# Last projection of a decoder layer: sixteen of twenty-two feature blocks by seven products of quarters, placed between the tiles of the projection before it

## The chip, the core and the metric

The kernel is one launch on one core of a Trainium2 chip. The core has a tensor engine (PE) for matmuls, with its weight loads (PEld) shown apart, a vector engine (DVE), a scalar or activation engine (ACT), a general engine (POOL) and a queue (SP) that issues the transfers between the chip's main memory and on-chip memory. Each engine works through its own list of instructions in the order in which they were issued; semaphores tie the lists together. The metric is device time in microseconds (us); lower is better.

## What is computed

One decoder layer on 512 tokens of width 1024, in float32: a gated mixer of three branches, and then a channel mixer (`conv_ffn`) whose two projections make up the last third of the kernel. The change concerns the second of these, `@ w_down`.

```python
def conv_ffn(u, w_up, conv_w, conv_b, w_down):
    h = causal_dwconv(u @ w_up, conv_w, conv_b)
    a, v = h[..., :D_FF], h[..., D_FF:]           # D_FF = 2816 = 22 blocks of 128
    return (jax.nn.silu(a) * v) @ w_down          # [512, 2816] @ [2816, 1024]

x = x + merged @ w_o[i]                           # the residual
x = x + conv_ffn(rmsnorm(x, ln2_g[i]), ...)
return rmsnorm(x, final_g)
```

## The kernel before

**Products in three parts.** Every float32 matrix is split into a high part (a cast by ACT, `fp32r`) and a low part (the rest, a subtraction by DVE). `mm3` (L230) then makes high x high, high x low, and low x high, in this order, over all the blocks of the contraction: 3 matmuls for each block. For a projection the tokens' block of 128 is loaded as weights and 512 columns stream past it.

**Jobs.** All work is cut into jobs, one tile of a weight matrix each. The program is written out by a generator; its order is the order on every engine. Before job n is issued, `prepare` (L1588) issues the low part of the weights of job n+1 (`lows`, L211, on DVE, then the job's `then`, if it has one), the cast of those of job n+2 (`cast`, L191, on ACT, in two halves, each at one of the job's steps), and the transfer of those of job n+3 (`fetch`, L179, on SP). There are 2 buffers for raw weights, 3 for high parts, 2 for low parts. A job calls `step()` at fixed places, usually twice; each step advances every generator in the list `running` by one stage. That is how work that belongs to an earlier tile gets laid between later ones.

**First projection of the channel mixer** (`up_jobs`, 22 jobs, numbered 0 to 21; even ones for a, odd ones for v, two blocks each, two products of 24 matmuls). `up_evac` takes each block out: ACT scales it (L1162), DVE adds the two taps of the convolution (L1165), ACT applies the silu to a (L1167), and POOL multiplies a and v (L1170). `later` then splits the result into its two parts, over the following steps. For the blocks below KS it makes more: each pair of blocks (2p, 2p+1) of tokens in two halves is a 2 x 2 matrix of quarters, and `sums_of` (L318 to L328) makes the four sums of quarters that seven products need, in three stages: four adds on DVE, two casts on ACT, two subtractions on DVE (`sl` or `sal`, then `sbl`). The sums are kept in `FS`, the plain parts in `ACTS`.

**Second projection** (`down`). For blocks 0 to 7 (KS = 8), seven products of quarters stand for eight, as in Strassen's method in Winograd's form. Four quarters of weights are read; differences of them (`diff`, L333) form the other three. The products, 24 matmuls each, are mixed with the plain jobs for blocks 8 to 21 (`blocks_of`). The products' results are added to one another and to the residual tiles `X1` (L1229, L1250, L1264, L1269, L1270). All of this runs after the last up job. `put_x1` writes the residual to main memory after up job 3, and `get_x1` reads it back before `down`.

**Memory.** `big` holds 54 tiles of 128 x 512 for everything in passing, PSUM has 4 banks under the name `mm` and 4 under `sm`.

Of the kernel before, what the change touches and what calls it, by code (L numbers as in the profile page):

```python
# [10 lines left out]
F32 = mybir.dt.float32  # L11
F32R = mybir.dt.float32r
# [4 lines left out]
P = 128  # L17
S = 512
# [10 lines left out]
SH = 16  # L29
DFF = 2816  # L30
KF = DFF // P
KS = 8
C_Q, C_K, C_V = 0, AW, 2 * AW
C_POOL = 3 * AW
C_Z = C_POOL + D
# [48 lines left out]
def trunk(ctx: ExitStack, tc, out, x, rel_bias, ln1_g, w_in, b_gate, w_a, pool_w, pool_scale, w_b,  # L84
# [26 lines left out]
    def MM(name):  # L111
        return psum.tile([P, S], F32, name=name, tag="mm")
# [970 lines left out]
                t = X1[tb, h] = T("x1")  # L1083
                sp.dma_start(t, x[tb * P:(tb + 1) * P, h * S:(h + 1) * S])

    def put_x1():
        nxt["x1"] = dram.tile([4, 2, P, S], F32, name="x1d")
        for tb, h in X1:
            sp.dma_start(nxt["x1"][tb, h], X1[tb, h])

    def get_x1():
        back = upool.tile([P, KD, S], F32, name="x1b", tag="ul")
        for h in range(2):
            for tb in range(4):
                X1[tb, h] = back[:, 2 * tb + h, :]
                sp.dma_start(X1[tb, h], nxt["x1"][tb, h])

    def wo_jobs(pair, h):
        def evac(tb, ps):
            t = X1[tb, h]  # L1100
# [33 lines left out]


    ACTS = {}
    wide = []
    ff = {}

    def ff_cols():  # L1140
# [19 lines left out]
    def up_evac(m, ps):  # L1160
        t = HC[m] = T("hc")
        act.activation(t, ps, AF.Identity, bias=ff["c1"][:, ff["b"] + m:ff["b"] + m + 1], scale=fw(2, m))  # L1162
        for k in range(2):
            sh = 2 - k
            dve.scalar_tensor_tensor(t[:, sh:], ps[:, :S - sh], fw(k, m), t[:, sh:], OP.mult, OP.add)  # L1165
        if m < KF:
            act.activation(t, t, AF.Silu)  # L1167
            return
        a = HC[m - KF]
        pool.tensor_tensor(a, a, t, OP.mult)  # L1170

        def later():
            yield
            k = m - KF
            if k >= KS or k % 2:
                h, l = T("fh", F32R), T("fl", F32R)
                act.copy(h, a)
                dve.tensor_sub(l, a, h.bitcast(F32))
                ACTS[k] = (h, l)
                if k < KS:  # L1180
                    yield
                    for _ in sums_of(HC[k - 1], a, *(t[:, k // 2, :] for t in wide),
                                     lambda j, h, l: FS.__setitem__((j, k // 2), (h, l))):
                        yield
                return
            if k == 0:
                wide.extend(ypool.tile([P, 4, S], F32R, name=n, tag="xs") for n in ("sh", "sl"))
            t = T("f0", F32R)
            act.copy(t[:, :256], a[:, :256])
            dve.tensor_sub(t[:, 256:], a[:, :256], t[:, :256].bitcast(F32))  # L1190
            FS[0, k // 2] = (t[:, :256], t[:, 256:])

        running.append(later())

    FS = {}

    def down():

        n2 = KS // 2
        quarter = lambda two, h: w_down[:KS * P, h * S:(h + 1) * S].rearrange(
            "(k two p) c -> two p k c", two=2, p=P)[two]
        W, acc, rs, r3 = {}, {0: {}, 1: {}}, {}, {}

        def load_w():
            both = upool.tile([P, KD, S], F32, name="w3", tag="uh")
            for at in range(2):
                W[at] = both[:, 4 * at:4 * at + 4, :]
                sp.dma_start(W[at], quarter(at, 1))  # L1210
            get_x1()

        def product(ps, ws, parts, first, last):

            wh, wl = ws
            mm3(ps, lambda k: wh[:, k, :], lambda k: wl[:, k, :], lambda k: parts[k][0],
                lambda k: parts[k][1], range(n2), first, last, flip=True)

        def first_half(i):
            return [[t[:, i * P:(i + 1) * P] for t in FS[0, p]] for p in range(n2)]  # L1220

        def second_half(tb):
            return [[t[:, tb * P:(tb + 1) * P] for t in ACTS[2 * p + 1]] for p in range(n2)]

        def sums(j, i):
            return [[t[:, i * P:(i + 1) * P] for t in FS[j, p]] for p in range(n2)]

        def add(tb, h, what):
            dve.tensor_tensor(X1[tb, h], X1[tb, h], what, OP.add)  # L1229

        def job(parts, use, form=None, ld=None):
            def body(ws):
                for i in range(2):
                    use(i, ws)
                    step()
            j = Job(parts, n2, S, body)
            j.form, j.load = form, ld
            return j


        def p2(i, ws):
            acc[0][i] = MM("pb")
            product(acc[0][i], ws, second_half(i), True, False)

        def p1(i, ws):
            ps = SM("p1")
            product(ps, ws, first_half(i), True, True)
            add(i, 0, ps)
            rs[i] = T("r1")
            act.copy(rs[i], ps)  # L1250
            if i:
                diff(W[0], W[1], W[0])

        def p5(i, ws):
            ps = SM("p5")
            product(ps, ws, sums(1, i), True, True)
            add(i, 1, ps)
            add(2 + i, 1, ps)

        def p7(i, ws):  # L1260
            ps = SM("p7")
            product(ps, ws, sums(3, i), True, True)
            r3[i] = T("r3")
            act.copy(r3[i], ps)  # L1264

        def p6(i, ws):
            ps = SM("p6")
            product(ps, ws, sums(2, i), True, True)
            dve.tensor_tensor(rs[i], rs[i], ps, OP.add)  # L1269
            dve.tensor_tensor(r3[i], r3[i], rs[i], OP.add)  # L1270

            def rest():
                yield
                add(2 + i, 0, r3[i])
                yield
                add(i, 1, rs[i])
                yield
                add(2 + i, 1, r3[i])
            running.append(rest())

        def p4(i, ws):
            product(acc[0][2 + i], ws, second_half(2 + i), False, True)
            add(2 + i, 0, acc[0][2 + i])
            running.append(early(2 + i))

        def p3(i, ws):
            acc[1][i] = SM("pb")
            product(acc[1][i], ws, sums(4, i), True, False)

        one = job([quarter(0, 0)], p1)  # L1290
        five = job([], p5, lambda: diff(one.raw, W[0], one.raw), lambda: None)
        def formed():
            diff(W[1], W[1], one.raw)
            return W[0]

        seven = job([], p7, formed, lambda: None)
        six = job([], p6, lambda: W[1], lambda: None)
        four = job([quarter(1, 0)], p4, lambda: diff(four.raw, four.raw, W[1]))
        plain = blocks_of(0, acc[0], (0, 1), (2, 3))

        yield Call(load_w)
        yield job([quarter(1, 0)], p2)
        yield next(plain)
        yield one
        yield five
        yield next(plain)
        yield seven
        yield next(plain)
        yield six
        yield from plain  # L1310
        yield four
        yield job([quarter(1, 1)], p3)
        yield from blocks_of(1, acc[1], (0, 1), ())

    def up_jobs():
        held = []
# [52 lines left out]
        yield  # L1369
        fin[tb] = norm_early(X1[tb, 0], fin["g"])  # L1370

    def blocks_of(h, acc, opened, keep):
        def evac(tb, ps):
            t = X1[tb, h]
            dve.tensor_tensor(t, t, ps, OP.add)
            if h == 0:
                running.append(early(tb))
                return
            v0, xg0 = fin[tb]
            for _ in norm_late(t, fin["g"], v0, lambda xg1: ((xg1, xg1), (xg0, xg0))):  # L1380
                xg1 = _
            for i, o in ((1, xg1), (0, xg0)):
                sp.dma_start(out[tb * P:(tb + 1) * P, i * S:(i + 1) * S], o)

        return jobs_b(lambda k0, k1: [wsrc(w_down, KS + k0, KS + k1, h * S, h * S + S)], S,
                      lambda k, tb: ACTS[KS + k][0][:, tb * P:(tb + 1) * P],
                      lambda k, tb: ACTS[KS + k][1][:, tb * P:(tb + 1) * P], KF - KS, evac,
                      mk=(MM, SM)[h], tail=2 if h else 0, acc=acc, opened=opened, keep=keep)


    class Call:
# [3 lines left out]
    def program():  # L1395
# [34 lines left out]
        for pair in range(2):  # L1430
            for h in range(2):
                yield from wo_jobs(pair, h)
            if pair == 0:
                yield Call(ff_cols)
        for i, job in enumerate(up_jobs()):
            yield job
            if i == 3:
                yield Call(put_x1)
        yield Call(lambda: fin.setdefault("g", grow(final_g)))
        yield Call(finish)  # L1440
        yield from down()

    jobs = list(program())
    weights = [j for j in jobs if isinstance(j, Job)]
# [166 lines left out]
ORDERED = {EngineType.PE, EngineType.Activation, EngineType.DVE, EngineType.Pool}  # L1611
NBIG = 54
MORE = 2
SPLIT = 4
MIX = "ZZ0zz1ggggaa"
SSD_ORDER = ((0, 0, 1), (1, 0, 1), (0, 1, 1), (2, 0, 1), (1, 1, 1), (3, 0, 1), (2, 1, 1), (3, 1, 1))
# [30 lines left out]
```

## Time and profile before

| | us |
|---|---|
| median of 3 runs | 1051.29 (1051.25 to 1051.93) |
| the profiled execution, as timed | 1052.9 |
| its span in the profile | 1050.8 |
| PE busy | 1037.0 (99%), 5220 matmuls |
| DVE busy | 642.9 (61%) |
| ACT busy | 467.4 (44%) |
| POOL busy | 137.7 (13%) |
| up jobs on the chain, from 699.47 | 229.42 |
| weights' low parts on DVE, L211 | 218.6 (95 instructions) |
| weights' high parts on ACT, L191 | 189.6 (188 instructions) |

Times in a row of the profile are microseconds from the start of the span, unless a row says ns. A row in order of time gives start, length, engine, line, operation, what is written and from what, and how many instructions are merged; in brackets how long the engine stood idle before it and on whom it waited. Where rows of one engine follow closely, they overlap a little in their ends: the distance from start to start is what an instruction costs in a dense row. A row by stages gives the stage, its length, the busy time of PE, PEld, DVE, ACT and POOL with counts, the clock granted to PE (1.00 is full), the share of the transfer engines and GB/s.

### The profile page before, as it was taken

What the parts mean: (1) busy time and instruction counts of PE and PEld (TensorE: products, weight loads), DVE (VectorE), ACT (ScalarE), POOL (GpSimd) and SP (SyncE); (2) the same over time, 40 slices, a digit from 0 to 9 for tenths busy, and PEclk for the clock granted to TensorE, in tenths of its full rate; (3) what the DMA queues carried; (4) which work ended last, traced back from release to release, by engine and by line L of the source; (5) the groups of instructions that cost most, each with busy time, mean ns of one, the idle gap of its engine ahead of it and who ended that gap; (6) DMA issues with size and microseconds to landing.
All of it is one profiled execution on the core that took longest, in us unless ns stands there. A gap on an engine that the chain in (4) does not pass through costs nothing.

```text
span 1050.8 us, 13095 instructions
## 1 busy us (share of the span) xinstructions
PE 1037.0 (99%) x5220; PEld 864.9 (82%) x5220; DVE 642.9 (61%) x867; ACT 467.4 (44%) x753; POOL 137.7 (13%) x118
## 2 busy tenths in 40 slices
PE   8999999999999999999999999999999999999997
PEld 8888877898888887787887888898888888878885
DVE  5563565675356657576658856766766556556545
ACT  5432544343474363566554324545444443433331
POOL 1670000000000001100143500001111111110110
PEclk9999999999999999999999999999999999999999
DMA  7544312026322354641252426653232322362322
GB/s 241 156 125 136 113 49 74 31 56 182 104 80 81 80 149 112 151 121 52 79 147 85 150 91 220 205 161 119 81 119 82 107 94 82 119 240 67 114 100 80
DMA packets 119787, 121.80 MB, mean 116 GB/s; under 512 B 5523, under 2 KB 101590, under 8 KB 119727
## 3 DMA queue, kind: packets, MB, share of 16 engines
q1 hardware_dynamic: 119727, 120.98, 37.4%
q8 instruction: 41, 0.67, 0.3%
q14 instruction: 19, 0.16, 0.0%
HBM read 115.07 MB, written 4.32 MB: 114 GB/s over the span
## 4 chain that ended last, share of the span: by engine, by line
PE 94%; DVE 3%; DMA 1%; ACT 1%; issue 1%; POOL 0%; SPq 0%; DVEq 0%; ACTq 0%; POOLq 0%
PE pa L230 32%; PE pu L230 22%; PE pb L230 17%; PE pqk L230 9%; PE pa L1507 2%; PE p L230 2%; PE ps L656 1%; PE pu L1329 1%; PE po L695 1%; PE pt L683 1%; PE ppw L230 1%; DVE wl L211 1%; PE py L955 1%; DMA raw<-in_w_in_dram 1%; PE pyo L961 1%
## 5 line engine op out<-in xcount | busy, mean ns | idle before, releaser
L211 DVE TENSOR_TENSOR wl<-raw,wh 128x2048 fp32r<-128x2048 f32 (+3 forms) x95 | 218.6, 2302 | 80.3 <-ACT wh L191 42.3
L191 ACT CAST wh<-raw 128x1024 fp32r<-128x1024 f32 (+3 forms) x188 | 189.6, 1026 | 68.5 <-DVE raw L333 21.1
L230 PE MATMUL pa<-uh,wh 128*128 128x512 f32 x384 | 98.8, 399 | 0.0
L1165 DVE SCALAR_TENSOR_TENSOR hc<-pu,fcol,hc 128x510 f32<-128x510 f32 x88 | 65.9, 748 | 50.8 <-ACT hc L1162 49.2
L230 PE MATMUL pa<-uh,wl 128*128 128x512 f32 x384 | 95.0, 390 | 0.3 <-DVE wl L211 0.3
L230 PE MATMUL pa<-ul,wh 128*128 128x512 f32 x384 | 95.0, 390 | 0.0
L230 PEld LDWEIGHTS pa<-uh,wl 128*128 128x128 f32 x384 | 72.0, 188 | 15.6 <-DVE wl L211 0.7
L230 PEld LDWEIGHTS pa<-ul,wh 128*128 128x128 f32 x384 | 72.1, 188 | 15.2
L230 PE MATMUL pu<-uh,wh 128*128 128x512 f32 (+1 forms) x352 | 83.7, 380 | 0.0
L230 PE MATMUL pu<-uh,wl 128*128 128x512 f32 (+1 forms) x352 | 83.5, 380 | 0.0
L230 PE MATMUL pu<-ul,wh 128*128 128x512 f32 (+1 forms) x352 | 83.5, 380 | 0.0
L230 PEld LDWEIGHTS pa<-uh,wh 128*128 128x128 f32 x384 | 70.2, 188 | 15.2 <-issue 1.0
L230 PEld LDWEIGHTS pu<-uh,wh 128*128 128x128 f32 x352 | 64.1, 188 | 12.7 <-ACT uh L448 0.2
L230 PEld LDWEIGHTS pu<-ul,wh 128*128 128x128 f32 x352 | 64.2, 188 | 12.5
L230 PEld LDWEIGHTS pu<-uh,wl 128*128 128x128 f32 x352 | 64.2, 188 | 12.5
L1162 ACT ACTIVATE hc<-pu,fcol,fcol 128x512 f32<-128x512 f32 x40 | 31.2, 779 | 75.4 <-PE pu L230 75.2
L1170 POOL TENSOR_TENSOR hc<-hc 128x512 f32<-128x512 f32 x22 | 31.5, 1430 | 223.5 <-DVE hc L1165 169.3
L934 POOL TENSOR_TENSOR xd<-xc,dec 128x512 f32<-128x512 f32 x6 | 6.4, 1063 | 364.0 <-DVE xc L925 345.4
L677 ACT ACTIVATE sb<-sb,nm 128x128 f32<-128x128 f32 (+1 forms) x72 | 30.1, 419 | 22.9 <-DVE nm L674 17.2
L1050 ACT ACTIVATE sg<-pa,col 128x512 f32<-128x512 f32 x24 | 16.5, 687 | 51.8 <-PE pa L230 51.7
L230 PE MATMUL pqk<-uh,wh 128*128 128x512 f32 x144 | 36.9, 394 | 0.0
L230 PE MATMUL pqk<-ul,wh 128*128 128x512 f32 x144 | 36.3, 390 | 0.0
(343 smaller groups left out, 1752.4 us busy)
## 6 DMA issues: line engine op xcount, KB each, us to landing
raw<-in_w_in_dram SPq DMA_DIRECT2D x25, 1024.0 KB
raw<-in_ffn_w_up_dram SPq DMA_DIRECT2D x22, 1024.0 KB
raw<-in_w_in_dram SPq DMA_DIRECT2D x20, 512.0 KB
raw<-in_ffn_w_down_dram SPq DMA_DIRECT2D x10, 1024.0 KB
raw<-in_w_o_dram SPq DMA_DIRECT2D x8, 1024.0 KB
raw<-in_w_b_dram SPq DMA_DIRECT2D x4, 1024.0 KB
al<-ad SPq DMA_DIRECT2D x16, 256.0 KB
raw<-in_w_c_dram SPq DMA_DIRECT2D x4, 1024.0 KB
```

Source lines behind the costliest of these rows:

```text
L191: act.copy(job.high[:, :, o], job.raw[:, :, o])
L211: (eng or dve).tensor_tensor(l[:, :, o], job.raw[:, :, o], h[:, :, o].bitcast(F32), OP.subtract)
L230: pe.matmul(ps, l, r, start=first and n == 0, stop=last and n == total - 1)
L656: pe.matmul(pss[i][:, o:o + w * P], q[r, n * P:(n + 1) * P], k[r, kb * P:(kb + w) * P], start=True, stop=True)
L677: act.activation(sb[:, off:off + w * P], sb[:, off:off + w * P], AF.Exp, bias=nm[:, n, h:h + 1], accum_out=ls[:, n, h:h + 1])
L683: pe.transpose(pt[:, o:o + P], sb[:, o:o + P], eye)
L695: pe.matmul(po[DH * hh:DH * hh + DH, n * P:(n + 1) * P], V[g, kb + i][:, (2 * c + hh) * DH:(2 * c + hh + 1) * DH], probs[2 * c + hh, nb][: ...
L1050: act.activation(s, ps, AF.Sigmoid, bias=col[:, o:o + 1])
L1162: act.activation(t, ps, AF.Identity, bias=ff["c1"][:, ff["b"] + m:ff["b"] + m + 1], scale=fw(2, m))
L1165: dve.scalar_tensor_tensor(t[:, sh:], ps[:, :S - sh], fw(k, m), t[:, sh:], OP.mult, OP.add)
L1170: pool.tensor_tensor(a, a, t, OP.mult)
L1507: pe.matmul(first[2 * n + j][:, lo:hi], a[:, k, j * P:(j + 1) * P], b[:, k, lo:hi], start=a is wh and b is uh and k == 0, stop=a is wl and ...
```

## The change

KS becomes 16: blocks 0 to 15 go by seven products, in two groups of eight blocks, and six blocks (16 to 21) stay plain. `down` is replaced by `down_group`, which makes one group's jobs. They are no longer put behind the up jobs: the list `AT` says after which up job each of them runs. Group 0 (blocks 0 to 7): product three after up job 9, seven after 10, one after 11, five after 12, six after 13, two and A22 after 14. Group 1 (blocks 8 to 15): after 17, 18, 19, 20, 21, and the last two after the first plain job. Each product's result is added in full to the residual tiles, from its own banks; `rest` spreads twelve of these adds over the steps behind six. The weights W are read three up jobs ahead of three into two buffers of `ypool`. The sums' parts get tiles of `big` instead of the two wide ones. `put_x1` and `get_x1` are gone: the residual stays in its eight tiles. The plain jobs are those for six blocks: for each half one job of four blocks and one of two.

```diff
-KS = 8
+KS = 16
...
-    def put_x1():
...
-    def get_x1():
...
                 if k < KS:
                     yield
-                    for _ in sums_of(HC[k - 1], a, *(t[:, k // 2, :] for t in wide),
+                    for _ in sums_of(HC[k - 1], a, T("sah", F32R), T("sal", F32R),
                                      lambda j, h, l: FS.__setitem__((j, k // 2), (h, l))):
                         yield
...
-    def down():
+    def down_group(base):
+        quarter = lambda two, h: w_down[base * P:(base + 8) * P, h * S:(h + 1) * S].rearrange(
             "(k two p) c -> two p k c", two=2, p=P)[two]
+        W, r1, r2, r5, r7 = [], {}, {}, {}, {}
+        def side(j):
+            ks = range(base, base + 8, 2)
+            if j == "A11":
+                return [FS[0, k // 2] for k in ks]
+            if j == "A12":
+                return [[t[:, LO] for t in ACTS[k + 1]] for k in ks]
+            if j == "A22":
+                return [[t[:, HI] for t in ACTS[k + 1]] for k in ks]
+            return [FS[j, k // 2] for k in ks]
+        def load():
+            for two in range(2):
+                W.append(ypool.tile([P, 4, S], F32, name="w3", tag="xs"))
+                sp.dma_start(W[two], quarter(two, 1))
...
+        def job(j, raw, form, use):
             def body(ws):
+                wh, wl = ws
+                parts = side(j)
                 for i in range(2):
+                    ps = SM("pd")
+                    o = slice(i * P, (i + 1) * P)
+                    mm3(ps, lambda k: wh[:, k, :], lambda k: wl[:, k, :],
+                        lambda k: parts[k][0][:, o], lambda k: parts[k][1][:, o], range(4), flip=True)
+                    use(i, ps)
                     step()
...
+        def keep(r, name):
+            def use(i, ps):
+                r[i] = T(name)
+                act.copy(r[i], ps)
+            return use
+        def p1(i, ps):
+            keep(r1, "r1")(i, ps)
             add(i, 0, ps)
+        def p5(i, ps):
+            keep(r5, "r5")(i, ps)
+            dve.tensor_tensor(r2[i], r2[i], ps, OP.add)
+        def p6(i, ps):
+            dve.tensor_tensor(r1[i], r1[i], ps, OP.add)
             def rest():
                 yield
+                dve.tensor_tensor(r7[i], r7[i], r1[i], OP.add)
+                add(i, 1, r1[i])
                 yield
+                add(i, 1, r2[i])
+                add(2 + i, 0, r7[i])
                 yield
+                add(2 + i, 1, r7[i])
+                add(2 + i, 1, r5[i])
             running.append(rest())
+        def then1():
+            diff(W[0], W[0], one.raw)
+            dve.tensor_tensor(W[1], W[1], one.raw, OP.add)
+        one = job("A11", quarter(0, 0), None, p1)
+        two = job("A12", quarter(1, 0), None, lambda i, ps: add(i, 0, ps))
+        three = job(4, None, lambda: W[1], keep(r2, "r2"))
+        three.then = lambda: diff(W[1], W[1], W[0])
+        one.then = then1
+        two.then = lambda: diff(two.raw, two.raw, W[1])
+        return load, [[three], [job(3, None, lambda: W[1], keep(r7, "r7"))], [one],
+                      [job(1, None, lambda: W[0], p5)], [job(2, None, lambda: W[1], p6)],
+                      [two, job("A22", None, lambda: two.raw, lambda i, ps: add(2 + i, 0, ps))]]
...
+        loads, groups = zip(*(down_group(base) for base in range(0, KS, 8)))
+        between = {at: group.pop(0) for group, ats in zip(groups, AT) for at in ats}
         for i, job in enumerate(up_jobs()):
             yield job
-            if i == 3:
-                yield Call(put_x1)
+            for load, ats in zip(loads, AT):
+                if i == ats[0] - 3:
+                    yield Call(load)
+            yield from between.get(i, ())
         yield Call(lambda: fin.setdefault("g", grow(final_g)))
         yield Call(finish)
-        yield from down()
+        plain = down_jobs(0)
+        yield next(plain)
+        yield from between.get(2 * (KF // 2), ())
+        yield from plain
+        yield from down_jobs(1)
...
+AT = ((9, 10, 11, 12, 13, 14), (17, 18, 19, 20, 21, 22))
```

More of the change, by code (lines that the diff above doesn't have):

```diff
@@ L1084, in load_x1 @@
                 sp.dma_start(t, x[tb * P:(tb + 1) * P, h * S:(h + 1) * S])
-    def put_x1():
-        nxt["x1"] = dram.tile([4, 2, P, S], F32, name="x1d")
-        for tb, h in X1:
-            sp.dma_start(nxt["x1"][tb, h], X1[tb, h])
-    def get_x1():
[L1092 to L1096, printed above, removed]
     def wo_jobs(pair, h):
@@ L1136, in trunk @@
     ACTS = {}
-    wide = []
     ff = {}
@@ L1185, in later @@
                 return
-            if k == 0:
-                wide.extend(ypool.tile([P, 4, S], F32R, name=n, tag="xs") for n in ("sh", "sl"))
             t = T("f0", F32R)
@@ L1195, in trunk @@
     FS = {}
-    def down():
-        n2 = KS // 2
-        quarter = lambda two, h: w_down[:KS * P, h * S:(h + 1) * S].rearrange(
+    def down_group(base):
+        quarter = lambda two, h: w_down[base * P:(base + 8) * P, h * S:(h + 1) * S].rearrange(
             "(k two p) c -> two p k c", two=2, p=P)[two]
[L1204 to L1226, printed above, removed]
@@ L1228, in add @@
         def add(tb, h, what):
             dve.tensor_tensor(X1[tb, h], X1[tb, h], what, OP.add)
-        def job(parts, use, form=None, ld=None):
+        def job(j, raw, form, use):
             def body(ws):
+                wh, wl = ws
+                parts = side(j)
                 for i in range(2):
-                    use(i, ws)
-                    step()
[L1236 to L1243, printed above, removed]
@@ L1245, in p1 @@
-        def p1(i, ws):
-            ps = SM("p1")
-            product(ps, ws, first_half(i), True, True)
-            add(i, 0, ps)
[L1249 to L1270, printed above, removed]
+                    ps = SM("pd")
[3 more added lines that the diff above has]
+                    use(i, ps)
@@ new lines, in body @@
+                    step()
+            new = Job([raw] if raw is not None else [], 4, S, body)
+            new.form = form
+            if raw is None:
+                new.load = lambda: None
+            return new
+        def keep(r, name):
[5 more added lines that the diff above has]
+            keep(r1, "r1")(i, ps)
+            add(i, 0, ps)
+        def p5(i, ps):
+            keep(r5, "r5")(i, ps)
+            dve.tensor_tensor(r2[i], r2[i], ps, OP.add)
@@ L1272, in rest @@
+        def p6(i, ps):
+            dve.tensor_tensor(r1[i], r1[i], ps, OP.add)
             def rest():
                 yield
-                add(2 + i, 0, r3[i])
+                dve.tensor_tensor(r7[i], r7[i], r1[i], OP.add)
+                add(i, 1, r1[i])
                 yield
-                add(i, 1, rs[i])
+                add(i, 1, r2[i])
+                add(2 + i, 0, r7[i])
                 yield
-                add(2 + i, 1, r3[i])
+                add(2 + i, 1, r7[i])
+                add(2 + i, 1, r5[i])
@@ L1279, in p6 @@
             running.append(rest())
[L1281 to L1311, printed above, removed]
@@ L1312, in down @@
-        yield job([quarter(1, 1)], p3)
-        yield from blocks_of(1, acc[1], (0, 1), ())
+        def then1():
[7 more added lines that the diff above has]
+        two.then = lambda: diff(two.raw, two.raw, W[1])
@@ L1370, in early, with down_jobs @@
         fin[tb] = norm_early(X1[tb, 0], fin["g"])
-    def blocks_of(h, acc, opened, keep):
+    def down_jobs(h):
         def evac(tb, ps):
@@ L1387, in blocks_of @@
                       lambda k, tb: ACTS[KS + k][1][:, tb * P:(tb + 1) * P], KF - KS, evac,
-                      mk=(MM, SM)[h], tail=2 if h else 0, acc=acc, opened=opened, keep=keep)
+                      mk=(MM, SM)[h], tail=2 if h else 0)
     class Call:
@@ L1434, in program @@
                 yield Call(ff_cols)
+        loads, groups = zip(*(down_group(base) for base in range(0, KS, 8)))
+        between = {at: group.pop(0) for group, ats in zip(groups, AT) for at in ats}
         for i, job in enumerate(up_jobs()):
             yield job
-            if i == 3:
-                yield Call(put_x1)
+            for load, ats in zip(loads, AT):
+                if i == ats[0] - 3:
+                    yield Call(load)
+            yield from between.get(i, ())
         yield Call(lambda: fin.setdefault("g", grow(final_g)))
-        yield Call(finish)
-        yield from down()
+        plain = down_jobs(0)
[3 more added lines that the diff above has]
+        yield from down_jobs(1)
     jobs = list(program())
```

## The prediction

> **What bounds the kernel now.** I read the page's first two parts, then the chain that ended last, then the vector engine's queue in order of time through one pair of up jobs, and last the places where the tensor engine stands still.
>
> ```profile
> span 1050.8 us, 13095 instructions
> ...
> PE 1037.0 (99%) x5220; PEld 864.9 (82%) x5220; DVE 642.9 (61%) x867; ACT 467.4 (44%) x753; POOL 137.7 (13%) x118
> ...
> PE 94%; DVE 3%; DMA 1%; ACT 1%; issue 1%; POOL 0%; SPq 0%; DVEq 0%; ACTq 0%; POOLq 0%
> ```
>
> The tensor engine (PE) bounds everything: it is idle for only 14 us. A matmul fewer is worth its full pitch, and every wait that reaches PE costs its full length. From the chain:
>
> ```profile
> 699.47 229.42 PE pu L230 x1056
> 928.89 5.46 PE pb L230 x24
> 934.38 2.25 DVE wl L211
> 936.67 9.36 PE pb L230 x40
> ...
> 967.79 5.44 PE p L230 x24
> ```
>
> The up jobs run without a gap; one product of quarters (24 matmuls) takes 5.44 us, so a matmul's pitch is 0.227 and an up job of 48 takes 10.88. The question is whether the vector engine (DVE), in strict order, can feed products put between up jobs. Its load in two pairs of up jobs, one with sums of quarters and one without (columns: PE, weight loads, DVE, ACT, POOL busy, clock, DMA):
>
> ```profile
> 743.00:765.00 22.00, 22.00 (x99) 18.22 (x98) 15.06 (x18) 10.42 (x15) 2.89 (x2) 1.00 0.31 98
> ...
> 831.00:853.00 22.00, 22.00 (x98) 18.21 (x97) 12.80 (x12) 9.40 (x13) 2.91 (x2) 1.00 0.29 96
> ```
>
> DVE is at 68% and 58% there. Next, that queue in order of time; an even job ends at 743.77, the odd job after it at 754.65:
>
> ```profile
> 744.21 0.69 DVE L1178 TENSOR_TENSOR fl<-hc,fh 128x512 fp32r<-128x512 f32 x1 [2.49 <-ACT fh L1177]
> 744.89 1.53 DVE L1165 SCALAR_TENSOR_TENSOR hc<-pu,fcol,hc 128x510 f32<-128x510 f32 x2
> 746.35 0.41 DVE L318 TENSOR_TENSOR sa<-hc 128x256 f32<-128x256 f32 x1
> 746.52 0.63 ACT L1167 ACTIVATE hc<-hc 128x512 f32<-128x512 f32 x1 [1.66 <-DVE hc L1165]
> ...
> 747.06 1.04 ACT L191 CAST wh<-raw 128x1024 fp32r<-128x1024 f32 x1
> ...
> 748.12 2.29 DVE L211 TENSOR_TENSOR wl<-raw,wh 128x2048 fp32r<-128x2048 f32 x1 [0.23 <-ACT wh L191]
> ...
> 750.34 1.53 DVE L1165 SCALAR_TENSOR_TENSOR hc<-pu,fcol,hc 128x510 f32<-128x510 f32 x2
> ...
> 751.02 0.62 ACT L324 CAST sh<-sa 128x512 fp32r<-128x512 f32 x1
> ...
> 754.65 1.98 PE L230 MATMUL pu<-uh,wh 128*128 128x512 f32 x8
> 754.85 0.78 ACT L1162 ACTIVATE hc<-pu,fcol,fcol 128x512 f32<-128x512 f32 x1 [2.68 <-PE pu L230]
> ...
> 755.66 1.53 DVE L1165 SCALAR_TENSOR_TENSOR hc<-pu,fcol,hc 128x510 f32<-128x510 f32 x2 [3.80 <-ACT hc L1162]
> ...
> 757.11 0.68 DVE L327 TENSOR_TENSOR sl<-sa,sh 128x512 fp32r<-128x512 f32 x1
> 757.34 1.60 POOL L1170 TENSOR_TENSOR hc<-hc 128x512 f32<-128x512 f32 x1 [4.06 <-DVE hc L1165]
> 757.71 1.78 DVE L328 TENSOR_TENSOR sbl<-sb,sbh 128x512 fp32r<-128x512 f32 x1
> ...
> 759.42 0.41 DVE L1190 TENSOR_TENSOR f<-hc,f 128x256 fp32r<-128x256 f32 x1
> 759.76 2.27 DVE L211 TENSOR_TENSOR wl<-raw,wh 128x2048 fp32r<-128x2048 f32 x1
> ```
>
> Here one sees the four steps by which `later` makes a pair's sums: fl in the next job's first step, the sums (L318) in its second, the casts (L324) in the first step of the job after that, the low parts (L327, L328) in that job's second step, behind its last evacuation (L1165). So the sums of blocks 6 and 7, whose v half is up job 7, end in job 9. Start to start, a pair of L1165 costs 1.46, fl 0.61, the sums with their four adds 1.5, a low part 0.6. L328 took 1.78 where POOL's product ran beside it.
>
> **The change part by part.** Matmuls: 16 blocks by 7 for 8 and 6 plain are 336 + 144 = 480, before 168 + 336 = 504. 24 fewer: -5.4 us.
>
> The seam: before, PE stood 0.5 us at 936.67 for the first plain block's low part. Now that job takes blocks 16 to 19, its low part is issued a job earlier; its wait goes (bounds -0.5 to 0). -0.5.
>
> Residual: 16 transfers of 256 KB leave the SP queue, none on the chain above. Eight of the 54 buffers of `big` stay taken; by the program's order I count 51 at most, in product six, so no tile should wait; a miss there would add to the bounds only.
>
> The products themselves bring DVE work: per group 7 low parts of weights, 4 differences of the same size, 22 adds; ACT 14 half casts and 8 copies. Prices, start to start:
>
> ```profile
> 990.92 0.68 DVE L1229 TENSOR_TENSOR x1b<-x1b,r 128x512 f32<-128x512 f32 x1
> 991.52 2.29 DVE L211 TENSOR_TENSOR wl<-raw,wh 128x2048 fp32r<-128x2048 f32 x1
> 993.72 1.28 DVE L1375 TENSOR_TENSOR x1b<-x1b,pb 128x512 f32<-128x512 f32 x2
> ```
>
> An add is 0.6, a low part 2.2. Over the first group with its six up jobs: 13 x 2.2 + 4 x 2.2 + 22 x 0.6 + 24 evacuations x 0.73 + three pairs' sums x 3.7 = 79 us against 103.4 of PE. On average it is covered by DVE's idle time; what counts is where it stands late. Four places, with T as the end of the job before.
>
> (a) Product three runs straight after up job 9 (the second group: after 17), and needs pair 3's (pair 7's) sbl as its 8th weight load: at T + 7 x 0.227 = T + 1.6. By the rows, with T = 754.65, sbl ends at 759.49 = T + 4.8: it lies behind that job's own last evacuation and sl, and beside POOL. Nothing in the change moves it. PE stands 3.3 us with 0.05 of signalling (from below 2.2, if POOL's product misses sbl and it takes 0.7 as at 216.56 further down). The group of the up stage's four sbl instructions says which:
>
> ```profile
> L328 DVE TENSOR_TENSOR sbl<-sb,sbh 128x512 fp32r<-128x512 f32 x4 | 7.1, 1783 | 0.0
> ```
>
> All four met POOL, so I take 3.3. Twice: +6.6. Behind the waiting matmul stand 16 more of three; DVE's next low part is then early.
>
> (b) What a stop of that length does besides. The trace has one like it, in the mixer's own product of quarters:
>
> ```profile
> 214.43 0.69 PE L230 MATMUL pb<-wh,sbl 128*128 128x384 f32 x3
> ...
> 216.56 0.68 DVE L328 TENSOR_TENSOR sbl<-sb,sbh 128x512 fp32r<-128x512 f32 x1
> ...
> 217.29 0.44 PE L230 MATMUL pb<-wh,sbl 128*128 128x384 f32 x1 [2.18 <-DVE sbl L328]
> ```
> ```profile
> 217.57:218.65 1.08, 1.08 (x6) 1.08 (x5) 1.08 (x1) 0.00 (x0) 0.00 (x0) 0.61 0.00 0
> 218.65:219.93 1.28, 1.28 (x6) 1.28 (x5) 1.28 (x2) 0.48 (x1) 0.00 (x0) 0.50 0.00 0
> ...
> 221.21:224.00 2.79, 2.79 (x17) 2.79 (x17) 0.00 (x0) 1.83 (x3) 0.00 (x0) 1.00 0.00 0
> ...
> 936.67:939.00 2.33, 2.33 (x10) 1.96 (x11) 2.29 (x2) 0.00 (x0) 0.00 (x0) 1.00 1.05 394
> ```
>
> After 2.18 us without work the granted clock was 0.61, then 0.50 until 221.21: lost 0.39 x 1.08 + 0.5 x 2.56 = 1.7 us. After the 0.5 us at 936.67 it stayed 1.00. So a stop of 3.3 costs 1.7 more (bounds 0 and 3.4, two such spells). Twice: +3.4. The Trainium skill ("TensorE: Matmul & The Clock Gate", section on HAM oscillation) warns only of gaps over about 3.4 us, which would leave this term out and make the sum 5.1 less with (c)'s; the 2.18 us row speaks against it.
>
> (c) The end of the first group. In product six, `rest` puts 12 adds over the next steps, in the same steps as the sums of blocks 12 and 13, and two's low part brings a difference. One row sets how a low part fares beside POOL:
>
> ```profile
> 844.38 1.61 POOL L1170 TENSOR_TENSOR hc<-hc 128x512 f32<-128x512 f32 x1 [4.06 <-DVE hc L1165]
> 844.76 3.38 DVE L211 TENSOR_TENSOR wl<-raw,wh 128x2048 fp32r<-128x2048 f32 x1
> ```
>
> Up job 13 ends at G. DVE: evacuation to G + 2.5, f to 2.8, up 14's low part beside POOL to 6.1 (5.0 without), r1, fl, r1 1.8, sums 1.5, two adds: G + 10.7, which is H + 5.3 if H is the end of six. Two's low part and difference: H + 9.7. Only then up 14's first evacuation, to 11.2. ACT waits for it with the silu (0.55), and behind that stand half a cast of A22's weights (1.0) and the two casts of sums (1.0), so that the second chunk (ready at 10.9) is taken by ACT from 13.7 and by DVE from 14.5 to 15.9. ACT's second half cast for A22 ends at 17.5; DVE has two low parts of sums 1.2, four adds 2.4, then A22's low part 2.2: H + 21.8. PE ends up 14 at H + 10.9 and two at H + 16.3; A22 finds its cast 1.2 late and, eight matmuls on (H + 18.1), its low part 3.7 late in all. Without the collision 2.6. Middle: +3.2, idle in two pieces, the longer about as long as the 2.18 above, so one spell of slow clock more: +1.7 (bounds 0 and 1.7).
>
> (d) Elsewhere. After one's low part two differences more (4.4) hold up 11's first evacuation to about 4 us late, but its bank is not wanted until the next up job; up 12's low part then ends 2.6 before its use. At the second group's end `finish` sets ten adds in a row (6.1) ahead of two's low part and difference; plain job and two give 16.3 us of cover against 18.6 of chain: A22 late by 0.5 (0 to 1.6). The last weights come in behind A22's low part: taken 0.3 (0 to 0.8). +0.8.
>
> Sum: -5.4 - 0.5 + 6.6 + 3.4 + 3.2 + 1.7 + 0.8 = +9.8 us, from the span 1050.8 to 1060.6. The profiled run was timed at 1052.9, 2.1 more than its span, and lies 1.6 above the median 1051.29 of the three runs; the shift set on the median gives 1061.1. A measurement here can tell about 0.2%, 2.1 us, from no change.
>
> **Rivals.** *The clock holds*: stops cost their length only, as the 0.5 us one did. 1061.1 - 5.1 = 1056.0. The one stop of over 2 us speaks against it. 14%. By the section of the Trainium skill's page "TensorE: Matmul & The Clock Gate" named above it would be so.
>
> *A22 is in time*: DVE's adds are interleaved better than I lay them out, only (a) and (b) stay: 1061.1 - 4.9 = 1056.2. For it: the 20% of DVE time that is left over; against: DVE has no gap from G + 1 to G + 13. 13%. With the clock holding as well: 1052.8, no change to tell; 5%.
>
> *Faster*: the steps of `later` run one earlier than I count, so that sbl lies behind the first chunk's evacuation of job 9 and ends before T. The point is T + 1.6; sooner than that, (a) and its clock vanish, and A22's wait, less ACT's casts, is about 2.3 with no full clock spell: 1051.3 - 5.9 + 2.3 + 0.8 = 1048.5. Against it stand the four steps seen in the rows; 7%.
>
> **The numbers.** The forecast with both its parts 58%: 1061.1, on its own from 1057 to 1066. 3% for worse (a buffer of `big` that waits, a fourth slow spell). The range takes in the two single rivals: 1053.5 to 1066. Faster 8%, same 7%, slower 85%.
>
> **What would show it.** In the new trace: 24 fewer matmuls; two waits of PE for sbl of about 3.3 us in the first product after up jobs 9 and 17, each followed by about 3.4 us at clock 0.5; a wait of A22 for its cast and low part; no wait at the seam; 4 MB less moved. It would be wrong if sbl is written before the odd job ends, if the clock stays 1.00, or if DVE shows gaps in up job 14.

## The result and the profile after

| | before | after |
|---|---|---|
| median, us | 1051.27 (4 runs, 1049.29 to 1051.93) | 1059.47 (4 runs, 1059.04 to 1060.68) |
| ratio | | 1.0081 (95% interval 1.0067 to 1.0094) |
| forecast | | 1061.1 (1053.5 to 1066.0) |
| the profiled execution, its span | 1052.9, 1050.8 | 1059.04, 1057.1 |

The change makes the kernel slower by 0.8%. The page of the changed kernel, its first part:

```profile
span 1057.1 us, 13082 instructions
...
PE 1033.4 (98%) x5196; PEld 861.0 (81%) x5196; DVE 682.3 (65%) x926; ACT 482.7 (46%) x779; POOL 135.2 (13%) x118
```

There are 24 matmuls fewer, as counted, and PE is busy 3.6 us less; yet the span is 6.3 longer. PE's waits over the whole span:

```profile
PE pd L230 <- DVE sbl L328: 6.2, 2, 3.1
PE pb L230 <- DVE sbl L328: 2.2, 1, 2.2
PE pd L230 <- DVE wl L211: 2.2, 1, 2.2
...
PE pd L230 <- ACT wh L191: 1.4, 1, 1.4
```

The second row is the mixer's, which stood before too. The three rows of `pd`, 9.8 us, are new; the seam's wait is gone. The two stops for sbl and A22's two stops, in order of time on PE (start, length, count; in brackets the idle time before):

```profile
798.00 0.84 PE L230 MATMUL pd<-wh,sbl 128*128 128x512 f32 x3
801.97 0.79 PE L230 MATMUL pd<-wh,sbl 128*128 128x512 f32 x1 [3.12 <-DVE sbl L328]
...
890.54 1.20 PE L230 MATMUL pd<-wh,fh 128*128 128x512 f32 x4 [1.36 <-ACT wh L191]
891.58 1.08 PE L230 MATMUL pd<-wh,fl 128*128 128x512 f32 x4
894.82 1.20 PE L230 MATMUL pd<-wl,fh 128*128 128x512 f32 x4 [2.16 <-DVE wl L211]
...
936.09 0.50 PE L230 MATMUL pd<-wh,sbl 128*128 128x512 f32 x1 [3.12 <-DVE sbl L328]
```

Three sbl matmuls run, the eighth of the product waits. What DVE did meanwhile, after up job 9 (its last matmul ends at 797.3):

```profile
798.11 1.53 DVE L1152 SCALAR_TENSOR_TENSOR hc<-pu,fcol,hc 128x510 f32<-128x510 f32 x2 [1.59 <-ACT hc L1149]
799.57 0.68 DVE L327 TENSOR_TENSOR sal<-sa,sah 128x512 fp32r<-128x512 f32 x1
800.16 1.75 DVE L328 TENSOR_TENSOR sbl<-sb,sbh 128x512 fp32r<-128x512 f32 x1
```

The job's own evacuation, then the other low part, then sbl, at 1.75 instead of 0.7 beside POOL. And the stages after the two stops for sbl (stage, its length, PE, PEld, DVE, ACT, POOL, the granted clock):

```profile
801.97:805.00 3.03, 3.03 (x7) 2.45 (x8) 2.48 (x2) 0.50 (x2) 0.00 (x0) 0.50 0.00 0
...
936.09:940.25 4.16, 4.16 (x18) 3.45 (x19) 3.36 (x3) 2.06 (x3) 0.00 (x0) 1.00 0.10 12
```

The first stop is followed by 3 us at half clock, 1.5 us lost; the second, of the same length to 0.01 us, by none (why, the last section tells). From the first full up matmul to the last add's start the chain took 344.5 us before (699.47 to 1043.98) and 350.4 after (698.67 to 1049.09): +5.9. Its terms as measured are -5.4 - 0.5 + 6.2 + 3.5 + 1.5 = +5.3; 0.6 is unassigned. The up stage began 0.8 earlier, and the end after the last add took 1.2 longer, both in parts where the same work is done.

### The profile page after: what moved, and what is told of

It reads as the page before. It is cut to its first block, busy times and chain, and to the rows that moved or that the text cites. A ratio compares the mean times of both kernels' runs of the same rounds, so it can differ in the third digit from the quotient of the medians.

```text
span 1057.1 us, 13082 instructions
## 1 busy us (share of the span) xinstructions
PE 1033.4 (98%) x5196; PEld 861.0 (81%) x5196; DVE 682.3 (65%) x926; ACT 482.7 (46%) x779; POOL 135.2 (13%) x118
## 4 chain that ended last, share of the span: by engine, by line
PE 93%; DVE 3%; DMA 1%; ACT 1%; issue 0%; SPq 0%; DVEq 0%; ACTq 0%
PE pa L230 35%; PE pu L230 21%; PE pb L230 12%; PE pqk L230 9%; PE pd L230 6%; PE pa L1466 2%; PE ps L656 1%; PE pu L1280 1%; PE po L695 1%; PE pt L683 1%; PE ppw L230 1%; DVE wl L211 1%; DMA raw<-in_w_in_dram 1%; DMA al<-ad 1%; PE py L955 1%; DVE hc L1152 1%
## 5 line engine op out<-in xcount | busy, mean ns | idle before, releaser
L211 DVE TENSOR_TENSOR wl<-raw,wh 128x2048 fp32r<-128x2048 f32 (+3 forms) x92 | 211.2, 2296 | 49.1 <-ACT wh L191 40.8
L191 ACT CAST wh<-raw 128x1024 fp32r<-128x1024 f32 (+3 forms) x182 | 183.5, 1026 | 58.6 <-DMA raw<-in_w_in_dram 20.4
```

Source lines behind the costliest of these rows:

```text
L191: act.copy(job.high[:, :, o], job.raw[:, :, o])
L211: (eng or dve).tensor_tensor(l[:, :, o], job.raw[:, :, o], h[:, :, o].bitcast(F32), OP.subtract)
```

## The experiments

The kernel before, timed beside the first four, took 1051.58. Times given are medians.

**Sums one step earlier.** Only the place of sbl in DVE's list moves.

```diff
                 if k < KS:
-                    yield
                     for _ in sums_of(HC[k - 1], a, T("sah", F32R), T("sal", F32R),
```

> The changed kernel with one yield less in later: the four adds of a pair's sums are issued in the step that makes fl, so casts and low parts come one step earlier, and sbl stands behind the first evacuation of up jobs 9 and 17 instead of the last. Theory (the waits set the loss): both waits for sbl (3.1 each) and the slow clock behind them go; A22's wait of 3.5 shrinks by about 1, since ACT's casts of sums leave up job 14. 1059.5 - 6.2 - 2.5 - 1 = about 1050. Rival (products between up jobs cost by crowding the vector engine and the transfers, wherever the sums stand): within 2 us of 1059.5.

Measured 1050.35, ratio 0.9987 (0.9978 to 0.9996). PE's waits:

```profile
PE pd L230 <- ACT wh L191: 1.5, 1, 1.5
...
PE pd L230 <- DVE wl L211: 1.0, 1, 1.0
PE pd L230 <- DVE sbl L328: 0.8, 2, 0.4
```

The stops for sbl fall from 3.12 to 0.41 each, A22's from 3.5 to 2.4, and 9.1 us of the changed kernel's 1059.47 go with one yield. The rest of 0.4 is POOL's again: sbl took 1.79 beside it.

**Product three reads another pair.** The order and the work stay; only the operand, and so part of what is computed, is another.

```diff
+            if j == 4:
+                return [FS[j, min(k // 2, base // 2 + 2)] for k in ks]
             return [FS[j, k // 2] for k in ks]
```

> The changed kernel, but product three of each group reads the sums of the group's third pair in the place of its fourth's, so that part of the computation is changed; the order and the work of all engines stay. Theory: only the two waits for sbl and the slow clock behind them go, A22's wait stays 3.5: 1059.5 - 6.2 - (1.6 to 3.4) = 1050 to 1051.7. Rival (DVE is late anyway, the next low part stops PE instead): a wait for wl of about 3 in the up jobs 10 and 18, and no more than 2 us gained.

Measured 1050.38, ratio 0.9991 (0.9980 to 1.0002). Its profile has no wait at product three, none in up jobs 10 and 18, and A22's two stops unchanged:

```profile
884.61 1.20 PE L230 MATMUL pd<-wh,fh 128*128 128x512 f32 x4 [1.35 <-ACT wh L191]
885.64 1.07 PE L230 MATMUL pd<-wh,fl 128*128 128x512 f32 x4
888.88 1.20 PE L230 MATMUL pd<-wl,fh 128*128 128x512 f32 x4 [2.17 <-DVE wl L211]
```

With DVE's list as it was, the two waits alone (and the slow clock that may follow) are worth 9.1 us: more than the whole loss. Crowding of DVE as such is not the cause.

**A22 of the first group after up job 15.**

```diff
-                      [two, job("A22", None, ...)]]
+                      [two], [job("A22", None, ...)]]
...
-AT = ((9, 10, 11, 12, 13, 14), (17, 18, 19, 20, 21, 22))
+AT = ((9, 10, 11, 12, 13, 14, 15), (17, 18, 19, 20, 21, 22, 22))
```

> The changed kernel with the first group's product A22 put after up job 15 instead of straight behind product two. Theory: A22's wait (1.4 for its cast, 2.2 for its low part) goes and nothing takes its place: 1059.5 - 3.5 = about 1056, a little less if a slow clock goes with it. Rival: the raw weights of two are held a job longer, the fetch of up job 16 waits for that buffer, and PE stops there instead: 1059 or more.

Measured 1053.25, ratio 1.0018 (1.0004 to 1.0032); ten runs between 1050.12 and 1056.23. Not the 1056 expected, and for a reason I had not thought of. The waits:

```profile
PE pd L230 <- DVE sbl L328: 3.1, 1, 3.1
PE pb L230 <- DVE sbl L328: 2.2, 1, 2.2
PE pu L230 <- DVE wl L211: 2.0, 1, 2.0
```

A22's two steps now fall between up jobs 15 and 16, so pair 7's sums are done two steps earlier and the second group's stop for sbl is gone too. In the other direction, A22's low part was late because DVE was; the next one, up job 15's own, is late in its place, by 2.0. So -3.5 - 3.1 + 2.0 = -4.6. The rest of the 6.2 is open: less half clock behind these stops, which would be the first thought, isn't what this profile shows. It has 6.8 us of it at the stop for sbl and 3.4 behind the one of 2.0; the profile of the changed kernel has 3.4 at its four stops in all.

**Both.**

> Sums one step earlier and the first group's A22 after up job 15, both edits above in one. Theory: all four waits go, and 24 matmuls fewer and no seam wait are left: 1051.3 - 5.9 = 1045.4, to 1047 with small leftovers; faster than the kernel before by about 0.5%. Rival (crowding): no faster than the kernel before.

Measured 1046.92, ratio 0.9957 (0.9941 to 0.9974): faster than the kernel before. One stop of 0.4 at the first product three and one of 0.9 for a low part are left.

**The residual's traffic put back.** The transfers of `put_x1` and `get_x1` are added again; the second writes a tile that nothing reads.

```diff
+            if i == 3:
+                yield Call(put_x1)
...
+        yield Call(get_x1)
         plain = down_jobs(0)
```

> The changed kernel, with the residual also written to main memory after up job 3 and read back into an unused tile after the last product six, as many transfers as before the change; the copy that is used stays on chip. Theory: the traffic is off the path, so within 1 us of the changed kernel's 1059.5. Rival: keeping the residual on chip is worth something, 2 us or more above 1059.5.

Measured 1059.36 (1057.49 to 1063.82; the kernel before, timed beside this and the next three: 1051.43). Keeping the residual on chip is worth nothing that these four executions, 6.3 us apart, can tell.

**The first group alone.** `KS = 8` and `AT = ((9, 10, 11, 12, 13, 14),)`.

> The changed kernel with KS = 8: only the first group goes by seven products, between the same up jobs; blocks 8 to 21 are plain, so PE has the 504 matmuls of the kernel before. Theory: no gain from matmuls, one wait for sbl of 3.1, A22's 3.5, the seam's 0.5 gone, slow clock 0 to 3.4: 1051.6 + 6.1 + about 1.7 = 1059, no better and no worse than both groups within 2 us. Rival (cost comes from crowding by both groups): about half the loss, 1055.

Measured 1056.1, ratio 1.0049 (1.0035 to 1.0063), 3 us less than expected. The stop for sbl is 3.12 as before, with slow clock in the profile, but A22's is not:

```profile
PE pd L230 <- DVE sbl L328: 3.1, 1, 3.1
...
PE pd L230 <- DVE wl L211: 0.4, 1, 0.4
```

With KS = 8 the pairs 4 to 6 need no sums. From up job 14 to A22, DVE has none of their adds (1.5 in the profile of the changed kernel) and low parts (1.2) to make and ACT no casts of them, and A22 is 0.4 late, not 3.5. So A22's stop in the first group needs the second group's sums; the adds of `rest` alone, which are there as before, don't make it.

**The adds of `rest` three steps later.**

```diff
             def rest():
-                yield
+                for _ in range(4):
+                    yield
```

> The changed kernel with the adds of rest started three steps later, so that ten of them leave the vector engine's list ahead of A22's low part. Theory: A22's wait of 3.5 falls to 0.6 (a cast 0.2 late, a low part 0.4), the two waits for sbl stay 3.1: about 1056.5. Rival: the wait is ACT's, whose silu waits behind two's difference; the cast stays 1.4 late and the whole wait above 2.

Measured 1057.0, ratio 1.0054 (1.0035 to 1.0072). From the up jobs on, PE waited:

```profile
PE pd L230 <- DVE sbl L328: 6.2, 2, 3.1
PE pb L230 <- DVE wl L211: 1.6, 1, 1.6
PE pd L230 <- DVE wl L211: 0.2, 1, 0.2
PE pd L230 <- ACT wh L191: 0.2, 1, 0.2
```

A22's stop falls from 3.5 to 0.4: taking the adds out of the list is enough, and ACT's cast, which waited behind DVE, comes in time with them but for 0.15. With the run before, it takes both, the adds and the second group's sums, to make this stop. But the same edit moves the second group's adds too, and there they push the last weights' low part 1.6 late.

**All waits.** Sums earlier, A22 after up job 15, adds later, and sbl ahead of the other low part:

```diff
-        dve.tensor_sub(al, sa, ah.bitcast(F32))
         dve.tensor_sub(bl, sb, bh.bitcast(F32))
+        dve.tensor_sub(al, sa, ah.bitcast(F32))
```

> Sums one step earlier, the first group's A22 after up job 15, and two edits more: sbl is subtracted ahead of sl, and the adds of rest start three steps later. Theory: the 0.4 left before product three and the 0.9 left in up job 16 go, and the mixer's own wait for sbl (2.2) gets 0.6 shorter: 1046.9 - 1.9 = 1045. Rival: the later adds only move the lateness to the next low part: 1046.5 to 1048.

Measured 1045.91, ratio 0.9950 (0.9936 to 0.9963). The stops named are gone, and the mixer's is 1.57; the new one at the end is there as in the run just told. Hence the last:

```diff
-                for _ in range(4):
+                for _ in range(1 if base else 4):
```

> The kernel with all four edits, but the adds of rest start three steps later in the first group only; in the second they start as in the changed kernel. Theory: the wait of 1.6 that the late adds put before the last weights' low part goes and no other wait over 0.3 is left from the first up job on: 1045.9 - 1.6 = 1044.3. Rival: the wait came from the transfer of the last weights, not from the adds, and stays: 1045.9.

Measured 1043.07 against 1050.74 before, ratio 0.9926 (0.9913 to 0.9940). The wait at the end was the adds', not the transfer's. Its waits over the whole span, of which none lies after the first up job begins (682.22):

```profile
PE pb L230 <- DVE sbl L327: 1.6, 1, 1.6
PE uT L1486 <- DVE diag L1490: 1.4, 2, 1.0
PE pa L1417 <- DVE relb L511: 1.1, 1, 1.1
PE pa L1469 <- ACT uh L1456: 0.4, 1, 0.4
PE pa L230 <- DVE wl L211: 0.2, 1, 0.2
```

So seven products for eight do pay here, 7.7 us, once nothing stands behind DVE. Of that, 5.9 is the matmuls and the seam; 0.6 is the mixer's shorter stop, which belongs to no part of the change under study. The other 1.2 would fit the slow clock that the mixer's stop brings in some executions at 2.18 and brought in neither profile at 1.57; that is not shown.

## Why the prediction was right, and where it was not

*Matmuls and seam, -5.9.* 5196 for 5220, and no wait at the first plain job. The last kernel, without waits, shows the gain.

*The residual, 0.* The run with the traffic put back shows no cost that its spread would let one see. That no tile of `big` waits is in keeping with the waits listed; it wasn't tried by itself.

*(a), sbl, +6.6.* Right in place and size: 3.12 each, +6.2. The operand swap takes it away, and the moved yield, a different edit, all but 0.4 of each.

*(b), the slow clock, +3.4, and +1.7 in (c).* The mechanism is there, the size was not: I charged each of three stops with 1.7; in the profile one of the three had it, 1.5. That is 3.6 too much for the profiled execution. I had taken one row of one execution for the rule; what decides it, the last section tells. Over their spans the other three executions had a lower mean granted clock (0.993 to 0.994, against 0.995 in the profiled one and 0.997 before), which would be more of it. The rival in which the clock holds was right for two stops and wrong for one.

*(c), A22, +3.2.* Measured 1.36 for the cast and 2.16 for the low part, 3.5, near the upper of my two ends (1.2 and 2.5, 3.7): the collision with POOL that set this end did happen, as up job 14's low part shows in the profile after:

```profile
869.96 1.33 POOL L1157 TENSOR_TENSOR hc<-hc 128x512 f32<-128x512 f32 x1 [4.15 <-DVE hc L1152]
870.06 3.38 DVE L211 TENSOR_TENSOR wl<-raw,wh 128x2048 fp32r<-128x2048 f32 x1
```

*(d), elsewhere, +0.8.* Wrong. I read `finish` as still standing behind the last up job, and the diff printed above shows it so, as a line that stays; the change removes that line. The second group's adds are therefore spread over plain job and product two, and A22 there and the last weights come in time: 0 instead of 0.8. That piling up adds at that place would cost is shown by the kernel with the later adds, 1.6.

*The sum as a whole.* For the profiled execution it is 3.5 too high, 1060.6 against 1057.1: -3.6 of clock, -0.4 of sbl, +0.3 of A22, -0.8 of (d), and +1.0 that no term foresaw (the 0.6 above and the 0.4 by which the end grew more than the start shrank). The forecast came out only 1.6 above the median. The profiled execution before lay 1.6 above its median, the one after 0.4 below, which no term foresaw; that much of the closeness is luck.

*Rival "faster".* I gave 1048.5 to sums one step earlier than I counted. Built, it ran at 1050.35: it keeps 0.4 of each stop for sbl, since sbl also then meets POOL, and 2.4 of A22's. The steps were counted right; the rival did not hold for the change as it stands.

## What to carry to other kernels

When work is laid between the tiles of a dense engine, take the list of the engine that feeds it and walk it in order around each seam: a share of busy time of 65% said nothing, and one yield was worth 9 us. Where a value is made in stages over steps, count the step in which its last instruction is issued, and what stands ahead of it there; the consumer must come a job later, or the value a step earlier. Moving a late engine's work is only a cure if the place it goes to has room: twice here the wait came back at the next low part.

## What the runs showed of the hardware

The same stop costs its length alone in one execution, and its length and 1.7 us more in another. The mixer's stop of 2.18 us is the same instruction with the same wait in nine of these profiles (before, after, and all experiments but the two with sbl first). Of the kernel where product three reads another pair, and of the changed kernel, PE in order of time:

```profile
216.09 0.44 PE L230 MATMUL pb<-wh,sbl 128*128 128x384 f32 x1 [2.18 <-DVE sbl L328]
216.37 0.86 PE L230 MATMUL pb<-wl,sbh 128*128 128x384 f32 x4
217.07 0.85 PE L230 MATMUL pb<-wh,sbh 128*128 128x384 f32 x4
217.76 0.85 PE L230 MATMUL pb<-wh,sbl 128*128 128x384 f32 x4
```

```profile
217.11 0.45 PE L230 MATMUL pb<-wh,sbl 128*128 128x384 f32 x1 [2.18 <-DVE sbl L328]
217.40 0.95 PE L230 MATMUL pb<-wl,sbh 128*128 128x384 f32 x4
218.15 1.48 PE L230 MATMUL pb<-wh,sbh 128*128 128x384 f32 x4
219.43 1.48 PE L230 MATMUL pb<-wh,sbl 128*128 128x384 f32 x4
```

In the first, four matmuls keep their 0.7 from start to start; in the second they take 1.28 for about 3.4 us. It was slow in five of the nine. Of the eight stops of 3.12 in all profiles, six were followed by half clock (for 3.4 us in four of them, for 6.8 in two: the one of the kernel with A22 after up job 15 and the first of the kernel with the later adds), and two of four between 2.0 and 2.2 at A22 or up job 16. Of the stops from 0.4 to 1.6 us behind the kernel's start none was.

The traces tell which. In each profile, up to the end of the span, the granted clock changes only at points that lie whole multiples of 3.41 us apart; in the changed kernel's at 218.00, 221.41, 801.68, 805.10 and 1054.27. Here is its trace cut into windows by these points; the figure behind the first comma is PE's busy time, the rest of the window is the time that it stood:

```profile
214.59:218.00 3.41, 1.23 (x7) 0.91 (x7) 3.41 (x4) 1.10 (x2) 0.00 (x0) 1.00 0.00 0
218.00:221.41 3.41, 3.41 (x13) 3.41 (x12) 2.39 (x2) 0.48 (x1) 0.00 (x0) 0.50 0.00 0
798.27:801.68 3.41, 0.57 (x3) 0.15 (x1) 3.38 (x4) 1.04 (x2) 1.55 (x1) 1.00 0.00 0
801.68:805.10 3.42, 3.13 (x7) 2.48 (x8) 2.77 (x3) 0.60 (x2) 0.00 (x0) 0.50 0.00 0
890.43:893.84 3.41, 2.12 (x8) 1.42 (x8) 3.38 (x5) 1.96 (x3) 0.00 (x0) 1.00 0.02 5
893.84:897.26 3.42, 2.44 (x11) 2.03 (x12) 3.38 (x6) 0.00 (x0) 0.00 (x0) 1.00 0.33 105
931.39:934.80 3.41, 1.57 (x7) 0.96 (x6) 2.53 (x4) 2.23 (x3) 1.59 (x2) 1.00 0.00 0
934.80:938.22 3.42, 2.13 (x9) 1.79 (x10) 3.42 (x3) 0.68 (x2) 0.69 (x1) 1.00 0.00 0
```

The mixer's stop and the first one for sbl leave PE without work for 2.18 and 2.84 us of one window, and the next window runs at half clock. The second stop for sbl, as long as the first, and A22's of 2.16 lie across a boundary, at most 1.84 us of them in one window, and the clock stays full. It is so in all eleven profiles, about 3300 windows: at full clock, no window in which PE stood for up to 1.86 us was followed by half clock, and every one in which it stood for 1.93 or more was. The two spells of 6.8 us had another 0.94 and 1.02 without work in their first slow window; after the windows with at most 0.29 full speed came back.

So the position of a stop in these windows decides, and they begin elsewhere in each profile: by these numbers at 214.59 here, at 215.52 in the kernel where product three reads another pair, though the two stops begin within 1 us. With the limit at about 1.9 us and every position as likely, an estimate is half clock for 0.5 of the stops of 2.18 ((3.41 + 2.18 - 2 x 1.9) / 3.41) and, in the same way, for 0.8 of those of 3.12; counted were five of nine and six of eight. So a stop of 2 to 3 us is to be priced at its length and about one us on the average: 13 of the 21 counted had a spell of half clock, and a spell costs about 1.7. Part of the spread between executions of one kernel would come from this: the kernel with A22 after up job 15, which keeps three such stops, the mixer's among them, ran from 1050.12 to 1056.23. No trace of its other executions shows that.

The Trainium skill ("TensorE: Matmul & The Clock Gate", section on the HAM clock gate) says that the gate looks at windows of about 3.4 us that run on whatever the kernel does. The traces agree, with changes of the clock at multiples of 3.41 us. Its advice to avoid gaps over 3.4 us does not warn of these stops, which are shorter and brought half clock from 2.00 us on.
